# Expert weights in 8 KB pieces with permuted features, the long overflow block moved to the sixth pair, and cross attention outputs formed as columns

## The chip, the cores and the metric

One core of a Trainium2 chip runs the whole program in one launch. The metric is device time in microseconds (us); the time shown for a kernel is the median of its runs. Durations of single instructions and transfers come from one profiled execution of the same kernel.

## The reference, cut to what matters

Two blocks run on one sequence of 256 tokens with 1024 features. The first has two layers, each a mixer followed by a mixture of 16 experts; the second has two layers of mixer, cross attention to 256 memory tokens with 4 heads, and a dense feed-forward part. The change touches the experts and the cross attention:

```
scores = sigmoid(t @ router_w)                      # t: (256, 1024) normalised
# best group of 4 experts, top 2 inside it, weights normalised to 1
for e in range(16):
    he = silu(t @ w_gate[e]) * (t @ w_up[e])        # 1024 -> 512
    y = y + combine[:, e:e+1] * (he @ w_down[e])    # 512 -> 1024
# cross attention, per head of 64
p = softmax(q @ k.T * 0.125)                        # 256 x 256
o = p @ v                                           # 256 x 64
out = concat(o) @ ca_wo                             # 256 -> 1024
```

The expert weights are 2 layers x 16 experts x 6 MB in float32, 201 MB in all. The kernel may not choose tokens ahead of time: which tokens an expert gets is known only after the router.

## The kernel before, in words

x (two tiles of 128 tokens) stays in SBUF. Dense products use a high and a low part of each operand (tiles ending in h and l, or hi and lo); the expert products use plain float32. Every large weight is read by SP's queue (`fetch`, L220 and L221) into slots of 1 MB that are used in rotation; an expert stage has 17 of them.

`moe` (L1214) handles 16 experts as 8 pairs. The two experts of a pair stand side by side in the columns of TensorE, with 64 token places each. First the tokens are normalised (`xn`), split into `xh` and `xl` by ACT (L1255) and POOL (L1256), and scored and ranked on DVE (L1271 to L1318). `prepare` makes, for two pairs at once, one-hot rows (`kept`, DVE, L1340) and gathers the tokens by products with xh and xl (`ph`, L1352); ACT applies the layer's scale and shift per feature (`hg`, L1356, with A and B, tiles moda and modc). `up(p)` multiplies by gate and up (`pg` and `pu`, L1399, 32 records each), scatters the pair before it back into x (`py`, L1419 and L1420, through `self.pending`; DVE adds at L1422), computes where its own tokens go (`places`: `pS`, `pw`, ACT L1372 and L1376), forms silu(pg) * pu on ACT and DVE (`hd`, L1407), transposes it on TensorE (`hT`, L183) and copies it out on DVE (`hidT`, L1412). For p = 1, 3, 5 it then prepares the next two pairs. `down(p)` multiplies by the down weights (`po`, L1432), scales on DVE (`of`, L1444) and splits for the scatter (`eo`, ACT L1447, DVE L1448).

Per pair, twelve transfers of 1 MB are issued (`weights`, L1520): four for gate, four for up, four for down. A piece is what one partition takes in one run of memory: with "(k p) n -> p k n" a row at a time, 2 KB for gate and up (rows of 512 values), 4 KB for down (rows of 1024).

An expert may get more than 64 tokens. From the third pair on, `If` blocks (L1545 and L1548) take up to 32 more per expert; `rounds` (L1509 to L1516) is five nested blocks for still more, thousands of instructions, and jumps over all of them for this data. It stands at p == 7, between the issue of pair 7's gate and up weights and that of its down weights, on PE, DVE, ACT and SP (L1511; the count is loaded at L1532). The order on each engine is the order of the code, apart from what a scheduler may move between pinned instructions.

`cross` (L2095) forms scores per head, exp on ACT (L2133), reciprocals of the sums (L2134), transposes P (`cpT`, copied to `pT` by ACT L196 or DVE L198), and multiplies with P transposed as the stationary side (`co`, L2154): rows of tokens, 64 columns per head. Then DVE scales by the reciprocal (`e`, L2158), `rows_T` transposes the result (`trr`) and splits it (ACT L630, DVE L631), and the output product follows (`op`, L380 to L382).

Of the kernel before, what the change touches and what calls it, by code (L numbers as in the profile page):

```python
# [119 lines left out]
class Net:  # L120
# [99 lines left out]
    def fetch(self, raw, src):  # L220
        self.nc.sync.dma_start(raw, src.rearrange("(k p) n -> p k n", p=P))  # L221
        return raw
# [973 lines left out]
    def router(self, l):  # L1196

        nc = self.nc
        V = nc.vector
        A, B = self.scale_shift(l, 1)  # L1200
        rwa = self.sp.tile([P, KD, NE], F32, tag="gt", name="rwa")
        self.rwp = self.sp.tile([P, KD, 2, NE], F32R, tag="e1", name="rwp")
        V.tensor_tensor(rwa, self.rw, A.unsqueeze(2).to_broadcast([P, KD, NE]), op=ALU.mult)
        hi, lo = self.rwp[:, :, 0, :], self.rwp[:, :, 1, :]
        self.tc.keep_in_program_order(nc.scalar.copy(hi, rwa))
        V.tensor_tensor(lo, rwa, hi.bitcast(F32), op=ALU.subtract)
        rwb = self.sp.tile([P, KD, NE], F32, tag="gt", name="rwb")
        V.tensor_tensor(rwb, self.rw, B.unsqueeze(2).to_broadcast([P, KD, NE]), op=ALU.mult)
        V.tensor_reduce(self.rb, rwb.rearrange("p k e -> p e k"), axis=AX.X, op=ALU.add)
        pb = self.bank([P, NE], name="rb")  # L1210
        nc.tensor.matmul(pb, self.k("ones"), self.rb, start=True, stop=True)
        V.tensor_copy(self.rb, pb)

    def moe(self, l):  # L1214
# [4 lines left out]
        with self.phase(f"moe{l}", MOE_RING, True) as mp:  # L1219
# [124 lines left out]
            def gather(oh, hg, k0=0, k1=KD):  # L1344
# [3 lines left out]
                for b0 in range(k0, k1, per):  # L1348
# [5 lines left out]
                    for b in range(per):  # L1354
                        k = b0 + b
                        nc.scalar.activation(hg[:, k, :], ph[:, b, :], AF.Identity,  # L1356
                                             scale=A[:, k:k + 1], bias=B[:, k:k + 1])
# [27 lines left out]
            def up(p, W):  # L1385
# [38 lines left out]
            def down(W, hidT, Sm, ws, last=False):  # L1424
# [13 lines left out]
                def back(n=4):  # L1438
# [20 lines left out]
            def more_up(p, r, W, hidT):  # L1459
# [22 lines left out]
                for k in range(4):  # L1482
                    self.tr(pt[:, k, :], hd[:, 128 * k:128 * k + 128])
# [25 lines left out]
            def rounds(r):  # L1509

                with tc.If(left > 32 + 32 * r):  # L1511
                    for rr, pp in [(1, e) for e in range(FIRST if r == 2 else 0)] + [(r, e) for e in range(8)]:
                        hidT = self.sp.tile([P, 4, 64], F32, tag="e2", name="hidTa")
# [6 lines left out]
            def weights(src, step, p, into=None):  # L1520
# [4 lines left out]
                t = [self.fetch(raw, w[j][k0:k0 + step, :]) for raw, (j, k0) in zip(into, cut)]  # L1525
                return t[0::2], t[1::2]

            for p in range(8):
                W = [weights("exp_w_gate", 512, p), weights("exp_w_up", 512, p)]
                self.spare = [self.slot([P, 2048]) for i in range(4)]  # L1530
                if p == 7:
                    left = nc.values_load(cnti[0:1, 0:1], min_val=0, max_val=2 * S,  # L1532
                                          engines=engines + (mybir.EngineType.SP,))
                    rounds(2)
                W.append(weights("exp_w_down", 256, p, self.spare))
# [559 lines left out]
    def cross(self, l):  # L2095
# [3 lines left out]
        with self.phase(f"ca{l}") as ap:  # L2099
# [9 lines left out]
            o = [self.bank([P, 256], name=f"co{t}") for t in range(2)]  # L2109
            rs = ap.tile([P, 2, 4], F32, name="rs4")  # L2110
# [11 lines left out]
            def scores(m):  # L2122
# [4 lines left out]
                for h, ps in zip((2 * m, 2 * m + 1), pp):  # L2127
# [6 lines left out]
                    V.reciprocal(rs[:, :, h], sm)  # L2134
                    st[h] = p

            def turned(m):
                for h in (2 * m, 2 * m + 1):
                    pt = self.bank([P, 2, 2, P], name="cpT")
                    for t in range(2):  # L2140
                        for j in range(2):
                            self.tr(pt[:, t, j, :], st[h][:, t, 128 * j:128 * j + 128])
                    st[h] = ap.tile([P, 2, 2, P], F32, tag="pT", name="pT", bufs=4)
                    self.copy(st[h], pt)

            def out(m):
# [9 lines left out]
            for t in range(2):  # L2156
                oo = self.sp.tile([P, 512], F32, tag="e1", name="e1")
                V.tensor_tensor(oo[:, 0:256].rearrange("p (h d) -> p h d", h=4), o[t].rearrange("p (h d) -> p h d", h=4),  # L2158
                                rs[:, t, :].unsqueeze(2).to_broadcast([P, 4, 64]), op=ALU.mult)
                self.rows_T(oo[:, 0:256], oT, 0, 2, t)  # L2160
                self.fill(2)
# [181 lines left out]
```

## Time and profile before

| what | value |
|---|---|
| median of 3 runs | 1603.82 us (1601.02 to 1606.61) |
| profiled execution | 1602.07 us, span 1600.3 us |
| PE busy | 1504.7 us, 94% |
| DVE, ACT, POOL busy | 887.1, 679.6, 121.4 us |
| weights' queue | 403.46 MB, 71.1% of the 16 engines' span |
| first expert stage | about 200 to 468 us |
| second expert stage | about 605 to 857 us |
| cross attention's ends | about 1024 to 1045 and 1381 to 1400 us |

A page row names the line, the engine and the operation, then output and inputs, the count, the busy time, the mean of one in ns, and the idle time of that engine ahead of it with what ended it. PE records overlap, so their busy times can add up to more than the stretch; where one engine's next instruction starts is the safer number.

### The profile page before, as it was taken

Reading aid. Unit: us, or ns where it says so; the run is one execution under the profiler, and the core shown is the slowest. Engines: PE = TensorE matmul, PEld = TensorE weight load, DVE = VectorE, ACT = ScalarE, POOL = GpSimd, SP = SyncE. Lnnn points to the kernel's source line nnn. Section 1 sums busy time; section 2 is a strip of 40 time slices with the busy share of each in tenths; the row PEclk is TensorE's granted clock in tenths of the full one; section 3 lists DMA queues with packets and bytes.
Section 4 is the critical chain, followed back from the end, with each engine's and each line's share of the span. In section 5 each row is a group of like instructions: output and inputs, shape, how many; then the busy total and the mean of one; then the engine's idle time right before and its main releaser. Section 6 shows DMA issues by size and latency. Waiting matters only on the chain. (4 is left out here: it accounts for less than half of the span.)

```text
span 1600.3 us, 23014 instructions
## 1 busy us (share of the span) xinstructions
PE 1504.7 (94%) x8845; PEld 1072.0 (67%) x8845; DVE 887.1 (55%) x1704; ACT 679.6 (42%) x1421; POOL 121.4 (8%) x170
## 2 busy tenths in 40 slices
PE   6999999999789999999978999999999999999998
PEld 3766644444349975444425887888887997888887
DVE  3755531122248984222116786766667776766666
ACT  3434421111035653101105355665556666665554
POOL 0320010000000002000001100110000211110000
PEclk9999999999889999999989999999999999999999
DMA  9998999989968799999998632554655542545640
GB/s 357 345 314 294 344 396 391 391 315 393 347 215 273 276 328 366 397 391 392 394 340 277 182 106 93 162 194 162 220 171 161 163 150 84 186 157 186 210 158 27
DMA packets 225758, 412.30 MB, mean 258 GB/s; under 512 B 7705, under 2 KB 91313, under 8 KB 225617
## 3 DMA queue, kind: packets, MB, share of 16 engines
q1 hardware_dynamic: 223040, 403.46, 71.1%
q0 software_dynamic: 2304, 6.98, 1.4%
q8 instruction: 86, 1.41, 0.4%
q14 instruction: 56, 0.45, 0.1%
q10 hardware_dynamic: 272, 0.00, 0.0%
HBM read 409.35 MB, written 1.06 MB: 256 GB/s over the span
## 5 line engine op out<-in xcount | busy, mean ns | idle before, releaser
L229 DVE TENSOR_TENSOR hl<-w,hl 128x1024 fp32r<-128x1024 f32 x280 | 337.2, 1237 | 49.8 <-ACT hl L228 49.4
L228 ACT CAST hl<-w 128x1024 fp32r<-128x1024 f32 x280 | 280.3, 1046 | 33.0 <-DMA w<-in_even_w_in 19.6
L2218 PE MATMUL pgu<-hT,hl 128*128 128x512 f32 x640 | 224.3, 394 | 0.0
L2219 PE MATMUL pgu<-hT,hl 128*128 128x256 f32 x640 | 177.1, 277 | 0.0
L380 PE MATMUL lin<-hl,hThi 128*128 128x256 f32 (+2 forms) x480 | 158.8, 334 | 2.0 <-ACT hl L228 1.3
L381 PE MATMUL lin<-hl,hThi 128*128 128x256 f32 (+2 forms) x480 | 153.6, 321 | 1.9 <-DVE hl L229 1.7
L382 PE MATMUL lin<-hl,hTlo 128*128 128x256 f32 (+2 forms) x480 | 153.1, 320 | 0.4 <-DVE hTlo L557 0.4
L2218 PEld LDWEIGHTS pgu<-hT,hl 128*128 128x128 f32 x640 | 119.9, 187 | 27.8
L1399 PE MATMUL pg<-w,hg 128*64 128x512 f32 x512 | 118.6, 615 | 19.7 <-ACTq L1545 9.2
L1407 DVE TENSOR_TENSOR hd<-hd,pu 128x512 f32<-128x512 f32 x16 | 11.0, 688 | 225.9 <-PE pu L1399 225.9
L1432 PE MATMUL po<-w,hidT 128*64 128x512 f32 x512 | 113.6, 595 | 10.0 <-DVEq L1548 5.8
L2219 PEld LDWEIGHTS pgu<-hT,hl 128*128 128x128 f32 x640 | 120.2, 188 | 2.0
L1399 PE MATMUL pu<-w,hg 128*64 128x512 f32 x512 | 114.9, 593 | 1.9 <-DMA w<-in_exp_w_up 1.9
L380 PEld LDWEIGHTS lin<-hl,hThi 128*128 128x128 f32 x480 | 92.3, 192 | 17.6 <-issue 8.1
L1399 PEld LDWEIGHTS pg<-w,hg 128*64 128x64 f32 x512 | 40.9, 141 | 93.4 <-issue 69.5
L381 PEld LDWEIGHTS lin<-hl,hThi 128*128 128x128 f32 x480 | 92.2, 192 | 11.0 <-DVE hl L229 3.5
L382 PEld LDWEIGHTS lin<-hl,hTlo 128*128 128x128 f32 x480 | 92.1, 192 | 8.0 <-issue 1.7
L1399 PEld LDWEIGHTS pu<-w,hg 128*64 128x64 f32 x512 | 41.1, 137 | 72.7 <-issue 68.0
L1432 PEld LDWEIGHTS po<-w,hidT 128*64 128x64 f32 x512 | 40.4, 137 | 72.8 <-issue 59.5
L1444 DVE SCALAR_TENSOR_TENSOR of<-po,ws,gate 128x512 f32<-128x512 f32 x32 | 23.9, 748 | 104.5 <-PE po L1432 100.6
L1447 ACT CAST eo<-of 128x512 fp32r<-128x512 f32 x32 | 19.8, 617 | 124.7 <-DVE of L1444 124.4
L380 PE MATMUL linc<-hThi,hl 128*128 128x256 f32 x224 | 66.8, 298 | 0.0
(554 smaller groups left out, 2915.0 us busy)
## 6 DMA issues: line engine op xcount, KB each, us to landing
w<-in_exp_w_gate SPq DMA_DIRECT2D x64, 1024.0 KB, 14.9
w<-in_exp_w_down SPq DMA_DIRECT2D x64, 1024.0 KB, 14.2
w<-in_exp_w_up SPq DMA_DIRECT2D x64, 1024.0 KB, 14.2
w<-in_ada_w SPq DMA_DIRECT2D x48, 1024.0 KB, 7.1
w<-in_ffn_wg SPq DMA_DIRECT2D x22, 1024.0 KB, 5.5
w<-in_ffn_wu SPq DMA_DIRECT2D x22, 1024.0 KB, 7.3
w<-in_ffn_wd SPq DMA_DIRECT2D x22, 1024.0 KB, 8.9
w<-in_even_w_in SPq DMA_DIRECT2D x14, 1024.0 KB, 10.1
```

What stands on the lines that cost most here:

```text
L228: pin(self.nc.scalar.copy(w[:, 0], src))
L229: pin(self.nc.vector.tensor_tensor(w[:, 1], src, w[:, 0].bitcast(F32), op=ALU.subtract))
L380: pin(mm(out, lh, rh, start=start, stop=False))
L381: pin(mm(out, lh, rl, start=False, stop=False))
L382: pin(mm(out, ll, rh, start=False, stop=stop))
L1399: pin(mm(pp[64 * j:64 * j + 64, :], hg[:, k, q][:, 64 * j:64 * j + 64], w[j][k // 4][:, k % 4, :], start=k == 0, stop=k == KD - 1, tile_po ...
L1407: V.tensor_tensor(hd, hd, pu, op=ALU.mult)
L1432: pin(mm(po[c][64 * j:64 * j + 64, :], hidT[:, k, 64 * j:64 * j + 64], W[2][j][k // 2][:, k % 2, 512 * c:512 * c + 512], start=k == 0, sto ...
L1444: V.scalar_tensor_tensor(of, po[c], ws, gate[:, cs], op0=ALU.mult, op1=ALU.mult)
L1447: nc.scalar.copy(eh[c], of)
L2218: mm(pp[i], wh[:, k, :], both[:, :, k, :], start=k == 0, stop=False)
L2219: mm(pp[i][:, 0, :], wl[:, k, :], hi[:, k, :], start=False, stop=k == KD - 1)
```

## The change

It has four parts. (1) The expert weights are read with "(p k) n -> p k n": a partition takes rows that follow one another, 8 KB in one piece, four rows of gate or up, two of down. So the order of the features along the partitions changes: xh and xl are written in that order by reads with a step of four, the scale and shift are laid out again through a DRAM tile `ab` by three POOL transfers, and the transposes of hd read with a step of two. (2) The scatter is split: two of its four products stand ahead of the transposes, two behind the copy, and `places` follows them. (3) `rounds` is called by `rest`, in pair 5 between the up and the down products, after gate and up of pair 6 have been issued; the order of the weight transfers is unchanged. (4) In the cross attention P is scaled by the reciprocal before it is transposed, V is the stationary side, and the output comes as columns (features on partitions) that are split at once by `finish`.

```diff
-    def fetch(self, raw, src):
-        self.nc.sync.dma_start(raw, src.rearrange("(k p) n -> p k n", p=P))
+    def fetch(self, raw, src, rows="(k p) n -> p k n"):
+        self.nc.sync.dma_start(raw, src.rearrange(rows, p=P))
...
+        flat = self.dram.tile([2, D], F32, name="ab")
+        for i, v in enumerate((A, B)):
+            nc.gpsimd.dma_start(flat[i].rearrange("(k p) -> p k", p=P), v)
+        self.ab = self.gp.tile([P, 2, 2, 4], F32, tag="ab", name="ab")
+        nc.gpsimd.dma_start(self.ab, flat.rearrange("i (b p k) -> p i b k", b=2, k=4))
...
-                    pin(nc.scalar.copy(xh[sl], xn[sl]))
-                    pin(nc.gpsimd.tensor_tensor(xl[sl], xn[sl], xh[sl].bitcast(F32), op=ALU.subtract))
+                    hi, lo = (e[sl].rearrange("p (k q) -> p k q", k=4) for e in (xh, xl))
+                    src = xn[sl].rearrange("p (q k) -> p k q", k=4)
+                    pin(nc.scalar.copy(hi, src))
+                    pin(nc.gpsimd.tensor_tensor(lo, src, hi.bitcast(F32), op=ALU.subtract))
...
                 if self.pending:
-                    self.pending()
-                Sm, ws = places([oh[t][:, q] for t in range(2)], p, 0)
+                    self.pending(2)
...
-                    self.tr(pt[:, k, :], hd[:, 128 * k:128 * k + 128])
+                    self.tr(pt[:, k, :], hd[:, 256 * (k // 2):256 * (k // 2) + 256].rearrange("p (q k) -> p k q", k=2)[:, k % 2, :])
                 hidT = self.sp.tile([P, 4, P], F32, tag="e2", name="hidT")
                 V.tensor_copy(hidT, pt)
+                if self.pending:
+                    self.pending(2)
+                Sm, ws = places([oh[t][:, q] for t in range(2)], p, 0)
...
+                t = [self.fetch(raw, w[j][k0:k0 + step, :], "(p k) n -> p k n") for raw, (j, k0) in zip(into, cut)]
...
+            def rest():
+                nonlocal left
+                W.extend(first_two(6))
+                self.spare = [self.slot([P, 2048]) for i in range(4)]
+                left = nc.values_load(cnti[0:1, 0:1], min_val=0, max_val=2 * S, engines=engines + (mybir.EngineType.SP,))
+                rounds(2)
...
                 own = up(p, W)
                 with tc.If(count > 64):
                     more_down(p, W, hidT, Sm, ws)
+                if p == 5:
+                    rest()
                 down(W, *own, p == 7)
...
-                    V.reciprocal(rs[:, :, h], sm)
+                    V.reciprocal(sm, sm)
+                    for t in range(2):
+                        V.tensor_scalar(p[:, t, :], p[:, t, :], sm[:, t:t + 1], None, op0=ALU.mult)
...
-                for h in (2 * m, 2 * m + 1):
-                    sl = slice(64 * h, 64 * h + 64)
-                    for t in range(2):
-                        for j in range(2):
-                            mm(o[t][:, sl], st[h][:, t, j, :], v[:, j, sl], start=j == 0, stop=j == 1)
+                o = self.bank([P, S], name="co")
+                for j in range(2):
+                    for b in range(2):
+                        h = 2 * m + b
+                        mm(o[64 * b:64 * b + 64, :], v[:, j, 64 * h:64 * h + 64], st[h][:, j, :], start=j == 0, stop=j == 1,
+                           tile_position=(0, 64 * b))
+                self.finish(oT, o, m)
```

PE in pair 6 of the first layer, from the up product to the branch ahead of the down product, before (pu is up, py the scatter, pS and pw the places, hT the transposes of hd):

```order
L1399 MATMUL pu<-w,hg 64x512 x16
L1419 MATMUL py<-eo,kept 128x512
L1420 MATMUL py<-eo,kept 128x512
...
L183 MATMUL pS<-kt,kept 128x128
L1365 MATMUL pw<-ch,kept 128x16
L1366 MATMUL pw<-cl,kept 128x16
...
L183 MATMUL hT<-kt,hd 128x128 x4
L1548 COMPARE_AND_BRANCH
```

The same stretch of PE in the changed kernel:

```order
L1409 MATMUL pu<-w,hg 64x512 x16
L1431 MATMUL py<-eo,kept 128x512
L1432 MATMUL py<-eo,kept 128x512
...
L183 MATMUL hT<-kt,hd 128x128 x4
L1431 MATMUL py<-eo,kept 128x512
L1432 MATMUL py<-eo,kept 128x512
...
L183 MATMUL pS<-kt,kept 128x128
L1375 MATMUL pw<-ch,kept 128x16
...
L1569 COMPARE_AND_BRANCH
```

The transposes moved from the end of the stretch to its middle; half of the scatter and the places now stand between them and the down product.

DVE in pair 5, before (kept is the one-hot rows for pairs 6 and 7, L1422 adds the scatter into x):

```order
L1407 TENSOR_TENSOR hd<-hd,pu 128x512
L1422 TENSOR_TENSOR x<-x,py 128x512 x4
L1340 TENSOR_TENSOR kept<-rk,kt 128x256 x2
L1412 COPY hidT<-hT 128x512
L1548 COMPARE_AND_BRANCH
```

and in the changed kernel:

```order
L1416 TENSOR_TENSOR hd<-hd,pu 128x512
L1434 TENSOR_TENSOR x<-x,py 128x512 x2
L1421 COPY hidT<-hT 128x512
L1434 TENSOR_TENSOR x<-x,py 128x512 x2
L1349 TENSOR_TENSOR kept<-rk,kt 128x256 x2
L1569 COMPARE_AND_BRANCH
```

The copy moved two additions ahead, and the one-hot rows now stand behind it.

PE behind the up part of pair 5 in the changed kernel (ph is the gather; L1569 is the small block, L1548 loads the count, L1523 is the long block):

```order
L1361 MATMUL ph<-kept,xl 128x256
L1569 COMPARE_AND_BRANCH
...
L1548 TENSOR_LOAD cnti
L1523 COMPARE_AND_BRANCH
...
L1523 UNCONDITIONAL_BRANCH x6
L1444 MATMUL po<-w,hidT 64x512 x16
```

Before, the small block was followed by the down product at once, and the long block stood behind the down product of pair 6.

## Rows read from the trace of the kernel before

**Rows 1.** The page: the up product's line, the gate weights' transfers.

```profile
L1399 PE MATMUL pu<-w,hg 128*64 128x512 f32 x512 | 114.9, 593 | 1.9 <-DMA w<-in_exp_w_up 1.9
...
w<-in_exp_w_gate SPq DMA_DIRECT2D x64, 1024.0 KB, 14.9
```

**Rows 2.** Windows: length, busy time of each engine, granted clock, DMA share, GB/s.

```profile
232.00:236.00 4.00, 4.00 (x22) 1.29 (x18) 0.00 (x0) 0.00 (x0) 0.00 (x0) 1.00 1.03 410
...
244.00:248.00 4.00, 4.00 (x22) 1.30 (x20) 0.00 (x0) 0.60 (x1) 0.00 (x0) 1.00 1.05 387
...
605.00:857.00 252.00, 227.95 (x1137) 106.11 (x1135) 67.97 (x130) 46.95 (x105) 7.52 (x8) 0.98 1.01 381
...
676.80:705.00 28.20, 27.07 (x128) 11.80 (x130) 8.05 (x13) 3.02 (x7) 0.00 (x0) 1.00 1.04 391
```

**Rows 3.** Timeline of PE, second expert layer, pairs 5 and 6: start, us, operation.

```profile
763.76 4.46 PE L1399 MATMUL pu<-w,hg 128*64 128x512 f32 x18
...
772.31 0.50 PE L1419 MATMUL py<-eo,kept 128*128 128x512 f32 x1
...
794.83 0.59 PE L1399 MATMUL pu<-w,hg 128*64 128x512 f32 x1
...
804.23 0.50 PE L1419 MATMUL py<-eo,kept 128*128 128x512 f32 x1
...
806.75 0.66 PE L183 MATMUL hT<-kt,hd 128*128 128x128 f32 x4
808.23 7.09 PE L1432 MATMUL po<-w,hidT 128*64 128x512 f32 x32 [0.83 <-DVEq L1548]
...
833.87 7.05 PE L1399 MATMUL pu<-w,hg 128*64 128x512 f32 x32
```

**Rows 4.** Timeline of ACT and PE around the long block, both layers.

```profile
435.49 9.48 PE L1399 MATMUL pg<-w,hg 128*64 128x512 f32 x32 [7.70 <-ACTq L1511]
...
816.52 0.62 ACT L1447 CAST eo<-of 128x512 fp32r<-128x512 f32 x1 [1.42 <-DVE of L1444]
...
824.53 9.52 PE L1399 MATMUL pg<-w,hg 128*64 128x512 f32 x32 [9.21 <-ACTq L1545]
```

**Rows 5.** Timeline of POOL, ACT and DVE at the first expert layer's start.

```profile
193.63 1.81 POOL L859 TENSOR_TENSOR x<-x,gt 128x512 f32<-128x512 f32 x1
...
199.92 1.13 ACT L1255 CAST xh<-xn 128x512 fp32r<-128x512 f32 x2
...
201.72 2.96 POOL L1256 TENSOR_TENSOR xl<-xn,xh 128x512 fp32r<-128x512 f32 x2
...
205.44 2.63 POOL L1256 TENSOR_TENSOR xl<-xn,xh 128x512 fp32r<-128x512 f32 x2 [0.76 <-ACT xh L1255]
205.58 1.36 DVE L1279 TENSOR_TENSOR ec<-sel 128x128 f32<-128x128 f32 x1
```

**Rows 6.** Timeline, first cross attention's end; last, instructions of L953 (ns min/median/max).

```profile
1034.32 3.82 PE L2154 MATMUL co<-kv,pT 128*128 128x64 f32 x32
...
1036.37 0.61 ACT L196 COPY pT<-cpT 128x512 f32<-128x512 f32 x1
...
1039.99 0.47 PE L380 MATMUL op<-hl,oTh 128*128 128x512 f32 x1
...
L953 DVE TENSOR_SCALAR p<-p,sm x64: 277/318/352, 142.5 to 991.6; 128x128 f32<-128x128 f32 x32, 128x256 f32<-128x256 f32 x32
```

**Rows 7.** Timeline of POOL ahead of the first expert layer.

```profile
192.37 3.07 POOL L859 TENSOR_TENSOR x<-x,gt 128x512 f32<-128x512 f32 x2 [60.94 <-DVE modc L793]
```

**Rows 8.** Timeline of PE and ACT, pair 5's gather; SP's waits, whole run.

```profile
775.96 0.39 PE L1352 MATMUL ph<-kept,xh 128*128 128x256 f32 x1 [0.47 <-DVE kept L1340]
...
777.31 4.03 ACT L1356 ACTIVATE hg<-ph,modc,moda 128x256 f32<-128x256 f32 x8 [1.78 <-PE ph L1352]
...
780.55 7.09 PE L1432 MATMUL po<-w,hidT 128*64 128x512 f32 x32 [0.40 <-ACT hg L1356]
...
SPq L1511 <- SPq L1511: 19.2, 4, 11.9
```

More of the change, by code (lines that the diff above doesn't have):

```diff
@@ L1356, in gather @@
                         nc.scalar.activation(hg[:, k, :], ph[:, b, :], AF.Identity,
-                                             scale=A[:, k:k + 1], bias=B[:, k:k + 1])
+                                             scale=self.ab[:, 0, k // 4, k % 4:k % 4 + 1],
+                                             bias=self.ab[:, 1, k // 4, k % 4:k % 4 + 1])
             def places(oh, p, r):
@@ L1436, in down, with back @@
                 order = [(c, t) for c in range(2) for t in range(2)]
-                def back(n=4):
+                def back(n):
                     for c, t in [order.pop(0) for i in range(n)]:
@@ L1482, in more_up @@
                 for k in range(4):
-                    self.tr(pt[:, k, :], hd[:, 128 * k:128 * k + 128])
+                    self.tr(pt[:, k, :], hd[:, 256 * (k // 2):256 * (k // 2) + 256].rearrange("p (q k) -> p k q", k=2)[:, k % 2, :])
                 nc.scalar.activation(hidT, pt[:, :, 0:64], AF.Silu)
@@ L1512, in rounds @@
                     for rr, pp in [(1, e) for e in range(FIRST if r == 2 else 0)] + [(r, e) for e in range(8)]:
-                        hidT = self.sp.tile([P, 4, 64], F32, tag="e2", name="hidTa")
                         more_down(pp, None, hidT, *more_up(pp, rr, None, hidT))
@@ L1524, in weights, with first_two @@
                 cut = [(j, k0) for k0 in range(0, w[0].shape[0], step) for j in range(2)]
-                t = [self.fetch(raw, w[j][k0:k0 + step, :]) for raw, (j, k0) in zip(into, cut)]
+                t = [self.fetch(raw, w[j][k0:k0 + step, :], "(p k) n -> p k n") for raw, (j, k0) in zip(into, cut)]
                 return t[0::2], t[1::2]
-            for p in range(8):
[L1529 to L1535, printed above, removed]
+            def first_two(p):
+                return [weights("exp_w_gate", 512, p), weights("exp_w_up", 512, p)]
+            def rest():
[4 more added lines that the diff above has]
+                rounds(2)
+            left, W = None, []
+            for p in range(8):
+                if p != 6:
+                    W = first_two(p)
+                    self.spare = None
+                W = W[-2:] + [weights("exp_w_down", 256, p, self.spare)]
                 if p == 7:
@@ L2108, in cross @@
             oT = ap.tile([P, 2, S], F32R, name="oTh"), ap.tile([P, 2, S], F32R, name="oTl")
-            o = [self.bank([P, 256], name=f"co{t}") for t in range(2)]
-            rs = ap.tile([P, 2, 4], F32, name="rs4")
             st = {}
@@ L2141, in turned @@
                         for j in range(2):
-                            self.tr(pt[:, t, j, :], st[h][:, t, 128 * j:128 * j + 128])
-                    st[h] = ap.tile([P, 2, 2, P], F32, tag="pT", name="pT", bufs=4)
-                    self.copy(st[h], pt)
+                            self.tr(pt[:, j, t, :], st[h][:, t, 128 * j:128 * j + 128])
+                    st[h] = ap.tile([P, 2, 2 * P], F32, tag="pT", name="pT", bufs=4)
+                    self.copy(st[h], pt.rearrange("p a b c -> p a (b c)"))
             def out(m):
@@ L2149, in out @@
                     self.split_ahead(4)
-                for h in (2 * m, 2 * m + 1):
-                    sl = slice(64 * h, 64 * h + 64)
-                    for t in range(2):
-                        for j in range(2):
-                            mm(o[t][:, sl], st[h][:, t, j, :], v[:, j, sl], start=j == 0, stop=j == 1)
-            self.pipe(2, (scores, turned, out), 2)
[L2156 to L2161, printed above, removed]
+                o = self.bank([P, S], name="co")
[5 more added lines that the diff above has]
+                self.finish(oT, o, m)
+            self.pipe(2, (scores, turned, out), 2)
             self.drain()
```

## The prediction

> **What bounds the kernel now.** I read the page's busy shares first, then windows over the expert stages, then the PE timeline pair by pair, and last ACT, DVE, POOL and SP at the places where PE stands still. PE is busy nearly all the span. The expert stages look different at first sight: in the second one the DMA share is 1.01 over 252 us [rows 2], so a reader would call it bound by the weights. The timeline corrects that. A stretch of 28.2 us inside it has PE busy 27.07 us beside a DMA share of 1.04: both are full, and what counts is who waits for whom. Stretches with gate/up traffic (2 KB pieces) move 387 GB/s, with down traffic (4 KB) 410 GB/s [rows 2]. A pair is 12.58 MB, so 32 us at the mean rate of 391; PE needs about 27.5 us of work for it. The transfers are therefore the slower side, but 17 slots are full when a layer starts, and the lead is eaten only at about 4.5 us per pair. The page's line of the up product has 1.9 us of waits for weights in all [rows 1], and the timeline places them in the second layer: the up product of pair 5 lasts from 763.76 to 772.31, 8.55 us, and of pair 6 from 794.83 to 804.23, 9.40 us, where the nominal product takes 7.05 [rows 3]: 1.50 + 2.35 = 3.9 us is all that weights cost in the expert layers. The other stops are a fixed wait of 0.83 us ahead of the down product for the transposed hidden rows [rows 3], the long block (9.21 us idle in the second layer, 7.70 in the first) [rows 4], the start of each layer, where DVE ranks while POOL splits [rows 5], and the end of each cross attention [rows 6].
>
> **The change part by part**, against the profiled execution (1602.07 us with 1600.3 of span; the median of the runs, 1603.82, stands 1.75 above it). Under 0.3%, 4.8 us, no difference can be told.
>
> *8 KB pieces.* Going from 2 to 4 KB raised the rate from 387 to 410. For 8 KB no row exists; the bounds are no gain over 2 KB (387) and another equal step (433). I take 420: a pair then takes 30 us, and the lead is eaten at 2.5 us per pair, 15 us over six pairs, half of what was eaten before. So PE stops waiting for weights: **-3.9 us**, and not more, because no other PE wait in these layers is for a weight. At the lower bound gate and up are no faster and the gain is 0. (The Trainium skill, DMA: Bandwidth & Descriptors, in its warning on three rates, lets the HBM side bind at about 358 GB/s for a core, whatever the piece. By it the pieces could gain nothing and this term would be 0. The trace disagrees: 410 was moved [rows 2].)
>
> *Strided reads at a layer's start.* xh and xl are now written from reads with a step of four elements: four ACT casts (0.56 us each) and four POOL subtractions (1.48 each, then 1.32) [rows 5]. The POOL pass counts, since DVE's ranking operations end when POOL's do: 1.36 us for 128x128, from 205.58 on. No strided POOL row exists. Bounds: nothing, and the slowest POOL pass of this size, 1.81 us [rows 5]. At 1.81 the first two end at 201.72 + 3.62 = 205.34, before the next pair starts; the next end at 205.44 + 3.62 = 209.06 instead of 208.07: +1.0 us on the path. ACT between 0 and twice its time, where two casts stand ahead of the router's cast: 0 to +1.1. I take +1.0 a layer, because the steps are small beside a POOL pass of over a microsecond: **+2.0 us** (0 to +4.2). (The Trainium skill, GPSIMD Engine Reference, Performance pitfalls for Q7 kernels, speaks against this edit: it charges reads with a byte step over 8 about half more per element. The step here is 16 bytes. By it the passes would take 2.2 and 2.0 us, POOL would end near 210.1, and this term would be about +4; no run here shows it yet.)
>
> *Transposes with a step of two.* Four per pair take 0.66 us [rows 3]. Bounds 0 and doubled, +0.66 x 16 = +10.6 us; I take 0, because what is strided is the stationary side, loaded beside the running product.
>
> *Three small POOL transfers per layer* (scale and shift to DRAM and back in the new order). POOL stands idle for 60.94 us ahead of L859 [rows 7], where they now stand, and their reader is the gather at 210, so 0. Without that cover a landing of microseconds would sit ahead of the router.
>
> *Order inside a pair.* Before: up product, four scatters, places, transposes, copy (PE waits 0.83), down product. After: two scatters, transposes, two scatters, places. The copy (0.69 us on DVE) now runs under two scatters and the places, which are 1.5 us of PE work. PE's way from 804.23 to 808.23 is 4.00 us; without the wait it is 2.52 (to the transposes at 806.75) + 0.66 = 3.2: -0.75 in pairs 2, 4, 6, 7, and about -0.5 in pair 0, where only the places are moved under the copy. In pairs 1, 3, 5 the gather of the next pair covers the copy already. There it costs: DVE's one-hot rows, for which the gather waits at 775.96 (0.47 us) [rows 8], now stand behind the copy, 0.65 us later. Per layer -4 x 0.75 - 0.5 + 3 x 0.65 = -1.55; both **-3.1 us**. Bounds: -5 if the one-hot rows are not late, +0.5 if the copy is late by both x additions.
>
> *The long block in pair 5 instead of ahead of pair 7.* It is never executed, but each engine jumps over it and must fetch code. Before, PE waited for ACT: in the second layer ACT ends its last cast at 816.52 + 0.62 = 817.14 and PE resumes at 824.53, 7.4 us later; the first layer's stop is 9.21 - 7.70 = 1.5 shorter behind the same work, so about 5.9 [rows 4]. After, PE's down product of pair 5 stands behind the block and waits for ACT again. ACT's last work ahead of it is the gather's scaling, which ends at 777.31 + 4.03 = 781.34, 0.8 after the time 780.55 at which the down product started [rows 8]. So the stop is 0.8 + 5.9 to 7.4, less 0.4 that was waited there anyway: 6.3 to 7.8. I take 7.7, against (7.70 + 9.21) / 2 = 8.45: **-1.5 us** for both layers (-4.5 to +2). SP stands 11.9 us at the block [rows 8]; a weight takes 14.9 us from issue to landing [rows 1], so its queue stays filled, and the lead at pair 5 covers the rest.
>
> *Cross attention.* Removed: 32 product records, 3.82 us, and behind them scaling, transposes, cast and subtraction, until the output product starts at 1039.99 [rows 6]. Added: eight scalings of P on DVE (0.35 us each, by the self attention's L953 [rows 6]), a cast and a subtraction per head pair. The last copy of P transposed is ACT's, from 1036.37 to 1036.98, behind other casts, so the last head's two scalings, 0.7 us ahead of its transposes, can be absorbed. Then come 8 records of 256 columns (about 0.9 us) to 1037.9. The output product can start with the first head pair's rows and meets the second's in time: 1037.8 instead of 1039.99, -2.2; two of them: **-4.4 us** (-6.5 if the last copy comes earlier, -1 if the scalings lie on the path).
>
> Sum: -3.9 + 2.0 - 3.1 - 1.5 - 4.4 = -10.9. 1602.07 - 10.9 = 1591.2 for a profiled execution, 1592.9 against the median: **1593 us**.
>
> **The rivals.**
> - *The expert layers are bound by transfers after all.* For it: share 1.01 to 1.04. Against it: PE busy 27.07 of 28.2. If so, 100.7 MB a layer at 420 instead of 391 would save 17 us a layer: 1603.8 - 34 - 4 = about 1566. Chance 0.04.
> - *Code fetch in mid-stream (slower).* In pair 5 the pages of the jump come through the same DMA engines as 8 KB pieces; before they met 2 KB pieces. Place: ACT's jump at the block. Price: from nothing (5.9 and 7.4 us, code fetched while weights were moving) to four times the wait, +18 us a layer; in the middle +9, which gives 1593 + 18 = 1611. It turns the change into no gain at +5.5 a layer and makes it slower beyond 0.3% from +7.9 on. Chance 0.14.
> - *The pieces give nothing and the strides cost the upper bound.* 0 + 4.2 - 3.1 - 1.5 - 4.4 = -4.8: 1599; with half the cross gain swallowed by the next stage's weight conversion 1601. For it: most terms are under 5 us and the pieces help only in two pairs of one layer. Chance 0.20.
> - *The forecast* keeps 0.62.
>
> **How the numbers follow.** Faster by over 0.3%: forecast and transfers, 0.66. Same: 0.20. Slower: 0.14. Range: the low end takes most of the bounds in favour (-5 pairs, -4.5 block, -6.5 cross, no stride cost, about -20): 1583. The high end goes through the no-gain rival into the lower part of the code-fetch one: 1606.
>
> **What would show it.** Right: no idle time of PE put down to an up weight; the wait of 0.83 us gone in pairs 2, 4, 6, 7; a stop of 7 to 8 us inside pair 5 and none before pair 7; the output product of the cross about 2.2 us earlier after the last P copy; rates near 420 GB/s in the gate/up windows. Wrong: POOL's xl passes at over 2 us with the gather's start 2 us later; jumps of over 12 us; transposes of over 1.2 us per pair; a weight wait in pairs 6 and 7 behind SP's stop.

## The result, and the profile of the changed kernel

The changed kernel takes 1620.62 us (median, 1617.97 to 1623.11); the kernel before, on the same chip, 1603.31. The ratio is 1.0112 with a 95% interval of [1.0099, 1.0126]: slower by about 17 us, where 10 us faster was forecast and 1606 was the end of the range. The profiled execution has a span of 1621.3 us, 21.0 more than before; it is the slowest of its four, so the table shows about 4 us more than the medians do.

Where the 21 us lie is seen by setting the same events of both timelines side by side:

| event (start, us) | before | after | later by |
|---|---|---|---|
| POOL's x addition ahead of the first expert layer | 192.37 | 200.99 | 8.6 |
| first gate product of that layer | 212.83 | 225.35 | 12.5 |
| end of its last down product | 462.87 | 474.07 | 11.2 |
| POOL's x addition ahead of the second expert layer | 601.83 | 628.63 | 26.8 |
| first gate product of that layer | 622.27 | 649.82 | 27.6 |
| end of its last down product | 851.95 | 873.47 | 21.5 |
| end of the span | 1600.3 | 1621.3 | 21.0 |

The expert layers' pairs gain, 1.3 us in the first and 6.0 in the second. Everything that is lost is lost in the two mixers ahead of them (8.6, and 26.8 - 11.2 = 15.6) and at the starts of the layers (3.9 and 0.8). The cross attentions, which were to gain 4.4, leave almost nothing in the last row.

Into the mixers the change puts POOL's three transfers per layer, and the larger pieces of the expert weights that are fetched early. The timeline of POOL in the changed kernel (start, us, operation, idle time ahead and what ended it); the first x addition answers to [rows 7]:

```profile
109.31 0.94 POOL L1204 DMA_DIRECT2D ab<-moda  x1
...
140.01 0.94 POOL L1204 DMA_DIRECT2D ab<-modc  x1
154.27 0.77 POOL L1206 DMA_DIRECT2D ab<-ab  x1 [13.31 <-DMA ab<-modc]
200.99 3.07 POOL L859 TENSOR_TENSOR x<-x,gt 128x512 f32<-128x512 f32 x2 [45.95 <-DVE modc L793]
...
555.55 0.96 POOL L1204 DMA_DIRECT2D ab<-moda  x1 [70.80 <-DVE moda L796]
587.04 0.91 POOL L1204 DMA_DIRECT2D ab<-modc  x1 [30.54 <-DVE modc L787]
599.36 0.77 POOL L1206 DMA_DIRECT2D ab<-ab  x1 [11.41 <-DMA ab<-modc]
```

POOL itself has time to spare, 45.95 us, as forecast. But a transfer of 4 KB takes 13 and 11 us to come back. What the DMA engines did meanwhile is in the windows of the changed kernel from 109 us on (length, busy time of PE, PEld, DVE, ACT, POOL, granted clock, DMA share, GB/s):

```profile
109.00:113.00 4.00, 3.29 (x19) 2.52 (x17) 1.46 (x3) 3.80 (x6) 2.31 (x3) 1.00 1.01 373
113.00:116.00 3.00, 2.06 (x11) 1.81 (x12) 2.79 (x6) 2.20 (x5) 0.90 (x1) 1.00 1.42 245
116.00:119.00 3.00, 2.73 (x15) 1.09 (x13) 3.00 (x3) 0.00 (x0) 0.76 (x1) 1.00 1.05 29
119.00:122.00 3.00, 0.00 (x0) 0.00 (x0) 1.76 (x5) 0.00 (x0) 0.00 (x0) 1.00 1.09 87
122.00:125.00 3.00, 1.11 (x4) 0.19 (x4) 0.00 (x0) 0.00 (x0) 0.00 (x0) 0.76 0.75 228
125.00:128.00 3.00, 3.00 (x9) 1.47 (x9) 0.00 (x0) 0.00 (x0) 0.00 (x0) 0.67 1.04 387
```

The share is 1.05 and 1.09, and the queues together move 29 and 87 GB/s: for some eight microseconds, from 115 to 123, the weights hardly move, and the 4 KB written in 1024 pieces of 4 bytes is all that is new there (the number of pieces follows from the access pattern; the trace doesn't list them). The stretch as a whole, and below it ten microseconds of the kernel before at the same place:

```profile
115.00:123.00 8.00, 3.73 (x20) 1.91 (x18) 5.55 (x9) 0.81 (x3) 1.66 (x1) 1.00 1.03 61
...
110.00:120.00 10.00, 10.00 (x52) 5.65 (x51) 7.87 (x12) 4.62 (x8) 2.69 (x2) 1.00 1.03 372
```

The same share goes with 61 and with 372 GB/s, so a full share is not bandwidth in use. Here is the weights' queue (packets, MB, share), from 110 to 113 and from 116 to 119 us:

```profile
q1 hardware_dynamic: 593, 1.18, 102.9%
...
q1 hardware_dynamic: 50, 0.09, 104.8%
```

The same 16 engines' time holds 593 packets of weights, 0.08 us each, and then 50, of 1.0 us each. So the full share of the second stretch is the weights' own packets, each about twelve times as long. PE has no work from 119 to 122. The weights that come late are those of the modulation. In the first mixer PE waits for them itself, in the second DVE does, which does the modulation there, and PE behind DVE (timelines of PE, of DVE, of PE in the changed kernel):

```profile
123.89 1.92 PE L758 MATMUL ada<-w,cT 128*32 128x512 f32 x4 [5.16 <-DMA w<-in_ada_w]
```

```profile
568.04 0.49 DVE L761 TENSOR_SCALAR adarow<-w,cT 128x512 f32<-128x512 f32 x1 [7.05 <-DMA w<-in_ada_w]
...
599.01 0.49 DVE L761 TENSOR_SCALAR adarow<-w,cT 128x512 f32<-128x512 f32 x1 [6.32 <-DMA w<-in_ada_w]
```

```profile
569.71 0.39 PE L382 MATMUL linc<-hThi,hl 128*128 128x256 f32 x1 [3.93 <-DVE hl L229]
...
600.01 0.39 PE L1630 MATMUL z<-us,nuinc 128*128 128x256 f32 x1 [3.29 <-DVE us L203]
```

PE's idle time grows from 15.1 to 22.6 us in the first mixer and from 5.5 to 13.6 us in the second: 7.5 of the 8.6 us, and 8.1 of the 15.6. The mean granted clock falls too, from 1.00 to 0.97 and from 0.95 to 0.93. The rest of the 15.6 was not taken apart.

The expert layers did much of what the forecast said. The page and the windows of the changed kernel, beside [rows 1] and [rows 2]:

```profile
L1409 PE MATMUL pu<-w,hg 128*64 128x512 f32 x512 | 112.9, 592 | 0.0
```

```profile
200.00:204.00 4.00, 4.00 (x19) 3.28 (x19) 2.90 (x8) 0.73 (x2) 3.01 (x2) 1.00 1.00 422
256.00:260.00 4.00, 4.00 (x22) 1.33 (x20) 0.00 (x0) 0.60 (x1) 0.00 (x0) 1.00 1.00 414
```

No up weight is waited for, and 8 KB pieces move 414 to 422 GB/s (taken: 420). The long block's stops are now inside pair 5, beside [rows 4]; the wait of 0.83 us ahead of the down product [rows 3] is 0.30 in a pair that doesn't prepare (PE's timeline: pair 5 of either layer, then pair 7 of the second):

```profile
414.55 10.05 PE L1444 MATMUL po<-w,hidT 128*64 128x512 f32 x32 [4.36 <-PEq L1523]
...
814.03 9.98 PE L1444 MATMUL po<-w,hidT 128*64 128x512 f32 x32 [7.13 <-PEq L1523]
...
866.38 1.08 PE L1444 MATMUL po<-w,hidT 128*64 128x512 f32 x4 [0.30 <-DVE x L1434]
```

4.36 + 7.13 = 11.5 us stand where 7.70 + 9.21 = 16.9 stood. The product behind each stop takes 10 us instead of 7.09; the clock granted from 814 to 824 is 0.70 of full speed, a mean between its two levels of 1.2 and 2.4 GHz, after PE had stood still. The same was so in the kernel before (9.48 and 9.52 us) [rows 4].

### The profile page after: what moved, and what is told of

Same layout as the page of the kernel before. It is cut to its first block, busy times and chain, and to the rows that moved or that the text cites. A ratio compares the mean times of both kernels' runs of the same rounds, so it can differ in the third digit from the quotient of the medians.

```text
span 1621.3 us, 22921 instructions
## 1 busy us (share of the span) xinstructions
PE 1510.8 (93%) x8805; PEld 1076.0 (66%) x8805; DVE 890.9 (55%) x1716; ACT 684.5 (42%) x1421; POOL 128.3 (8%) x176
## 5 line engine op out<-in xcount | busy, mean ns | idle before, releaser
L2238 PEld LDWEIGHTS pgu<-hT,hl 128*128 128x128 f32 x640 | 119.8, 187 | 26.5
L1444 PE MATMUL po<-w,hidT 128*64 128x512 f32 x512 | 119.5, 620 | 15.3 <-PEq L1523 11.5
L1409 PE MATMUL pg<-w,hg 128*64 128x512 f32 x512 | 114.0, 596 | 3.4 <-PEq L1566 3.4
L1382 ACT CAST kept<-pS 128x256 fp32r<-128x256 f32 x17 | 6.3, 373 | 146.2 <-PE pS L183 146.2
## 6 DMA issues: line engine op xcount, KB each, us to landing
w<-in_exp_w_up SPq DMA_DIRECT2D x64, 1024.0 KB, 13.6
```

The costliest lines, as they stand in the source:

```text
L1409: pin(mm(pp[64 * j:64 * j + 64, :], hg[:, k, q][:, 64 * j:64 * j + 64], w[j][k // 4][:, k % 4, :], start=k == 0, stop=k == KD - 1, tile_po ...
L1444: pin(mm(po[c][64 * j:64 * j + 64, :], hidT[:, k, 64 * j:64 * j + 64], W[2][j][k // 2][:, k % 2, 512 * c:512 * c + 512], start=k == 0, sto ...
L2238: mm(pp[i], wh[:, k, :], both[:, :, k, :], start=k == 0, stop=False)
```

## The experiments

Theory: the 4-byte writes take the DMA engines from the weights, and that is the whole loss of the mixers. Rivals: the transfers are hidden, as forecast, and the 8 KB pieces, the block or the strides cost it. Times stand beside the kernel before on the same chip (1602.2 to 1602.5 us).

**1. The transfers alone.** The kernel before with these lines added; nothing reads `ab`.

```diff
+        flat = self.dram.tile([2, D], F32, name="ab")
+        for i, v in enumerate((A, B)):
+            nc.gpsimd.dma_start(flat[i].rearrange("(k p) -> p k", p=P), v)
+        self.ab = self.gp.tile([P, 2, 2, 4], F32, tag="ab", name="ab")
+        nc.gpsimd.dma_start(self.ab, flat.rearrange("i (b p k) -> p i b k", b=2, k=4))
```

> The kernel before, with nothing added but the three POOL transfers per layer that lay the scale and shift out again (two writes of 1024 pieces of 4 bytes to DRAM, one read back); their result is used by nothing. Theory: each of the two writes holds the DMA engines for about 10 us, the dense weights of the mixer come late, and PE stands for them; from the trace of the changed kernel this is 8.6 us in the first mixer and 15.6 in the second, so about 1603 + 24 = 1627 us (1618 to 1632). Rival (the forecast's own step: the transfers are hidden): 1603 within 3 us.

1629.17 us against 1602.38, ratio 1.0165 [1.0146, 1.0184]: +26.8 us. Three transfers of some kilobytes per layer cost more than the whole change loses. Its windows show the same stretch as the changed kernel's, with pieces of the old size, so 8 KB pieces have no part in it:

```profile
113.00:116.00 3.00, 1.49 (x9) 1.34 (x10) 2.77 (x6) 2.40 (x6) 0.34 (x1) 1.00 1.57 322
116.00:119.00 3.00, 3.00 (x18) 1.56 (x16) 3.00 (x4) 0.37 (x2) 1.32 (x1) 1.00 0.89 29
119.00:122.00 3.00, 0.31 (x1) 0.00 (x1) 2.33 (x5) 0.00 (x0) 0.00 (x0) 1.00 1.18 96
```

**2. The number of pieces.** As 1, but the same bytes go out as 128 pieces of 32 bytes.

```diff
-            nc.gpsimd.dma_start(flat[i].rearrange("(k p) -> p k", p=P), v)
+            nc.gpsimd.dma_start(flat[i].rearrange("(p k) -> p k", p=P), v)
```

> As the kernel with the three POOL transfers alone (1629 us), but each write to DRAM goes out in 128 pieces of 32 bytes instead of 1024 pieces of 4 (the same bytes, count of transfers and waits; the features then lie in another order, in a tile that nothing uses). Theory (the cost goes with the number of tiny pieces): two writes of about 10/8 us each per layer, at most +4 us, 1602 to 1606. Rival (the DRAM round trip and its waits on POOL's queue cost, whatever the pieces): 1620 or more.

1607.72 us against 1602.20, ratio 1.0031 [1.0021, 1.0040]: +5.5, a fifth of 26.8, with the same three transfers. A little over the expected 4. POOL's idle time ahead of the read back fell with it, from 12.7 and 11.8 us to 5.6 and 5.5. These windows of 3 us behind the first write don't fall below 227 GB/s:

```profile
108.00:111.00 3.00, 3.00 (x19) 2.52 (x16) 0.85 (x2) 2.80 (x4) 2.57 (x3) 1.00 1.00 340
111.00:114.00 3.00, 1.34 (x11) 1.00 (x10) 2.57 (x4) 2.50 (x4) 0.00 (x0) 1.00 1.06 400
114.00:117.00 3.00, 3.00 (x18) 2.24 (x20) 2.79 (x5) 1.20 (x3) 1.66 (x1) 1.00 1.03 383
117.00:120.00 3.00, 3.00 (x16) 0.99 (x9) 2.97 (x6) 0.00 (x0) 0.00 (x0) 1.00 0.75 227
```

So it is the tiny pieces that cost, not the round trip through DRAM. The run changes their number and their size together (and which pieces lie side by side in DRAM), and doesn't tell these apart.

**3. One write instead of two.** The kernel before with the scale's write alone, no read back.

```diff
+        flat = self.dram.tile([2, D], F32, name="ab")
+        for i, v in enumerate((A,)):
+            nc.gpsimd.dma_start(flat[i].rearrange("(k p) -> p k", p=P), v)
```

> The kernel before with one single write of 1024 pieces of 4 bytes per layer (the scale alone) and no read back; the result is used by nothing. Theory (each such write costs its 10 us of weights' transfer, and the path follows): half of the 26.8 us, 1614 to 1617. Rival (it is the wait of the read back on POOL's queue, or only the second write, that costs): 1602 to 1606.

1623.04 us against 1602.46, ratio 1.0135 [1.0110, 1.0160]: +20.6, three quarters and not half. The mechanism holds (no read back, no second write, and POOL's x addition still comes at 203.35 instead of 192.37, while in experiment 1 it came at 202.21), but the price is not per write. In the first mixer the first write costs everything and the second nothing: the second, at 141 us, falls where the weights have slack (208 GB/s from 150 to 160 us in the kernel before). In the second mixer the first costs about 10 us, and the second, with the read back, 4 more. What a stopped queue costs depends, by these places, on how soon PE needs what is in it.

**4. The change whole, laid out again without a transfer.** Sixteen small products (32 records in the trace) with columns of the identity bring scale and shift, which stand side by side in `both`, into the new order.

```diff
-        flat = self.dram.tile([2, D], F32, name="ab")
-        for i, v in enumerate((A, B)):
-            nc.gpsimd.dma_start(flat[i].rearrange("(k p) -> p k", p=P), v)
...
-        nc.gpsimd.dma_start(self.ab, flat.rearrange("i (b p k) -> p i b k", b=2, k=4))
+        eye = self.k("ident").rearrange("p (q k) -> p k q", k=4)
+        for g in range(4):
+            src = both.rearrange("p i (b g) -> p g i b", g=4)[:, g]
+            for k in range(4):
+                nc.tensor.matmul(pab[32 * g:32 * g + 32, :, :, k], eye[:, k, 32 * 0:32], src, start=True, stop=True,
+                                 tile_position=(0, 32 * g))
...
+        V.tensor_copy(self.ab, pab)
```

> The changed kernel whole, but scale and shift are laid out again by 16 small TensorE products with columns of the identity and one copy, with no transfer. Theory (the 4-byte writes cost 24 us): 1620.6 - 24 = about 1597 us (1592 to 1602), faster than the kernel before. Rival (8 KB pieces in the shared queue delay the mixers' weights, or the pieces are late themselves): 1612 us or more.

1600.26 us against 1602.38, ratio 0.9986 [0.9975, 0.9997]: 19 us better than the change, each against the kernel before on its own chip, and a little faster than before. The rival falls. But -2.1 is not the -10.9 of the forecast, so other terms were off too. The mixers now take 2.3 us (the first) and 1.4 us (the second) more than before instead of 8.6 and 15.6; of that the products are 1.45 us:

```profile
192.04 1.45 PE L1209 MATMUL pab<-both,kt 128*32 128x4 f32 x32
```

and the starts of the expert layers (from POOL's x addition to the first gate product) are 2.6 and 3.7 us longer. Two things make them longer. DVE, counted from the x addition, has its first one-hot rows ready 1.2 and 1.5 us later, because it waits longer for ACT, whose doubled casts stand ahead (first layer, before and here):

```profile
201.56 0.69 DVE L203 TENSOR_TENSOR hTlo<-tr,hThi 128x512 fp32r<-128x512 f32 x1 [0.44 <-ACT hThi L202]
...
204.82 0.69 DVE L203 TENSOR_TENSOR hTlo<-tr,hThi 128x512 fp32r<-128x512 f32 x1 [1.45 <-ACT hThi L202]
```

The other 3.6 us go with the clock. The windows of the first start, before, here, and with the long block alone (below), which changes nothing in a start:

```profile
192.37:212.83 20.46, 17.05 (x119) 12.31 (x117) 14.97 (x43) 8.64 (x22) 9.73 (x8) 1.00 1.04 395
194.71:217.72 23.01, 18.84 (x119) 13.32 (x117) 15.70 (x42) 10.61 (x22) 10.36 (x8) 0.93 1.01 422
193.20:215.01 21.81, 18.39 (x118) 13.23 (x116) 14.96 (x43) 8.64 (x22) 9.73 (x8) 0.92 1.04 395
```

A start at 0.92 is 1.4 us longer with nothing in it changed, and the second start here is at 0.87. Whether a start meets the lower level differs from one profiled execution to the next, and no run shows what decides it.

**5. The start of a layer.** As 4, but DVE, which writes the normalised tokens anyway, writes them in the new order, so ACT and POOL read without a step.

```diff
-                rs[t] = self.norm_rows(self.x, t, xn, t)
+                rs[t] = self.mean_square(self.x, t)
+                V.tensor_scalar(xn[:, t, :].rearrange("p (c k q) -> p c k q", c=2, k=4),
+                                self.x[:, t, :].rearrange("p (c q k) -> p c k q", c=2, k=4), rs[t], None, op0=ALU.mult)
...
-                    pin(nc.scalar.copy(hi, src))
-                    pin(nc.gpsimd.tensor_tensor(lo, src, hi.bitcast(F32), op=ALU.subtract))
+                    pin(nc.scalar.copy(xh[sl], xn[sl]))
+                    pin(nc.gpsimd.tensor_tensor(xl[sl], xn[sl], xh[sl].bitcast(F32), op=ALU.subtract))
```

> The kernel with all parts and scale and shift laid out on TensorE (1600.3 us), but DVE writes the normalised tokens in the permuted order, so ACT's casts and POOL's subtractions read without a step. Theory (ACT's doubled casts are what makes the start longer): casts back to 0.56 us, DVE's pass from 0.75 to at most 1.1 us, 1.5 us less per layer: 1597 (1595.5 to 1599). Rival (the start is longer for another reason, or DVE's pass takes what ACT gains): 1600 to 1602.

1596.20 us against 1602.20, ratio 0.9960 [0.9944, 0.9975]: 4 us better than experiment 4, where 3 were expected. The instructions of tile xn, first in the changed kernel, then in this one (count, ns min/median/max):

```profile
L1264 ACT CAST xh<-xn x8: 1099/1119/1132, 208.5 to 640.4; 128x512 fp32r<-128x512 f32 x8
L1265 POOL TENSOR_TENSOR xl<-xn,xh x8: 1502/1533/1771, 210.3 to 642.1; 128x512 fp32r<-128x512 f32 x8
```

```profile
L1268 ACT CAST xh<-xn x8: 602/610/615, 203.5 to 614.8; 128x512 fp32r<-128x512 f32 x8
L1269 POOL TENSOR_TENSOR xl<-xn,xh x8: 1292/1328/2179, 205.3 to 616.2; 128x512 fp32r<-128x512 f32 x8
L1274 DVE TENSOR_SCALAR xn<-x,rstd x4: 1197/1510/1852, 200.3 to 611.7; 128x1024 f32<-128x1024 f32 x4
```

ACT's cast takes 1.12 us with the step and 0.61 without; POOL's pass 1.53 and 1.33. DVE's two passes per layer became longer than expected: 1.20 and 1.8 us, where the kernel before took 0.75 and 1.4 (the second runs beside POOL). The whole still gains, but not all of the 4 us is shown to come from the casts. The first one-hot rows are ready 0.6 and 0.7 us earlier than in experiment 4. The two starts together are 4.9 us shorter; the other 3.6 go with the clock, which is 1.00 in both starts here. The run with the long block put back (below) has the same instructions at its starts, 0.92 in both, and 1.4 us more in each. Over whole runs the granted clock was 0.980 to 0.983 here and 0.976 to 0.980 in experiment 4; that the edit raised it isn't shown.

**6. The products in PE's idle time.** As 5, with the sixteen products moved from ahead of the mixer's output products to the start of the expert layer, where PE waits for the ranking; ACT copies the result.

```diff
             self.warm(WARM[2])
+            pab = self.bank([P, 2, 2, 4], name="pab")
...
             parts(1)
+            self.ab = self.gp.tile([P, 2, 2, 4], F32, tag="ab", name="ab")
+            pin(nc.scalar.copy(self.ab, pab))
```

> As the kernel in which DVE writes the permuted order (1596.2 us), but the 16 small TensorE products that lay scale and shift out stand in the expert layer's start, where TensorE waits for the ranking, and ACT copies their result; before, they stood ahead of the mixer's output products and took 1.6 us of TensorE there. Theory: 1.6 us less per layer, 1593 us (1592 to 1595). Rival (they are not on the path, or they delay the ranking's products): 1596 or more.

1592.79 us against 1602.46, ratio 0.9931 [0.9916, 0.9946], as expected (1593): 9.7 us faster than the kernel before, 27 faster than the change (each against the kernel before on its own chip), and the best version of this study. That all of the 3.4 us against experiment 5 come from the move isn't shown; the two intervals touch.

**7 to 11. The parts by themselves.** The cross attention alone (the last three pieces of the diff, in the kernel before):

> The kernel before with the cross attention's part of the change alone. The forecast: -4.4 us (1599). Theory from the trace of the changed kernel (the last head's two scalings wait behind two copies on DVE, and its transposes behind products of the other heads, so the output product gains 0.6 us in the first cross and not 2.2): -0.5 to -3 us (1600 to 1603).

1600.98 us, ratio 0.9988 [0.9978, 0.9999]: -1.4 of the forecast -4.4. Its timeline, beside [rows 6]:

```profile
1035.37 0.67 DVE L198 COPY pT<-cpT 128x512 f32<-128x512 f32 x1
1035.96 0.61 DVE L2134 TENSOR_SCALAR p<-p,sm 128x256 f32<-128x256 f32 x2
...
1036.45 0.41 PE L183 MATMUL cpT<-kt,p 128*128 128x128 f32 x2 [1.15 <-DVE p L2134]
1036.79 1.51 PE L2155 MATMUL co<-pT,kv 128*64 128x256 f32 x10
1038.23 0.44 PE L183 MATMUL cpT<-kt,p 128*128 128x128 f32 x2
1038.71 0.59 ACT L196 COPY pT<-cpT 128x512 f32<-128x512 f32 x1 [0.41 <-PE cpT L183]
1039.34 1.08 PE L2155 MATMUL co<-pT,kv 128*64 128x256 f32 x6 [0.68 <-ACT pT L196]
...
1040.35 0.50 PE L380 MATMUL op<-hl,oTh 128*128 128x512 f32 x1
```

The last head's scalings stand on DVE behind two copies of earlier heads, PE waits 1.15 us for them, and the last two transposes stand on PE behind ten records of the product. In the forecast these lay under ACT's late copy. From ACT's last copy to the output product it is 1.64 us, where [rows 6] have 3.62, so that part of the forecast (-2.2) nearly came; but the copy itself comes later by PE's wait.

The long block alone (`rest` called in pair 5, pieces as before):

> The kernel before with the long block moved into pair 5 alone, pieces and order within a pair unchanged. The forecast: -1.5 us. Theory from the trace of the changed kernel (stops of 4.0 and 6.8 us in pair 5 instead of 7.7 and 9.2 ahead of pair 7): -4 to -6 us (about 1598). Rival (code pages wait behind weights, SP's stop leaves the weights of pairs 6 and 7 late): slower than 1603.

1601.09 us, ratio 0.9991 [0.9980, 1.0002]: -1.3, near the forecast's -1.5, a gain that the interval doesn't quite separate from none. The stops were not the 4.0 and 6.8 us that were expected from the changed kernel:

```profile
404.60 8.97 PE L1432 MATMUL po<-w,hidT 128*64 128x512 f32 x32 [7.40 <-PEq L1511]
...
790.36 8.94 PE L1432 MATMUL po<-w,hidT 128*64 128x512 f32 x32 [7.34 <-PEq L1511]
```

14.7 us against 16.9 before: so the move alone shortens the stops by 2.2 us, and the first layer's short stop of 4.36 us comes only together with the rest of the change. Up weights were waited for longer, 4.1 us on the page's line of the up product against 1.9 [rows 1]: in the second layer, where weights are late, the shorter stops gained nothing (229.65 us from the first gate to the last down product, against 229.68). That a shorter stop gives late weights less time to catch up fits this, and is not tested by itself. So the other way round, from experiment 5 with the block put back:

```diff
+                if p == 7:
+                    left = nc.values_load(cnti[0:1, 0:1], min_val=0, max_val=2 * S,
+                                          engines=engines + (mybir.EngineType.SP,))
+                    rounds(2)
...
-                if p == 5:
-                    rest()
```

> As the kernel in which DVE writes the permuted order (1596.2 us), but the long block is back ahead of pair 7. Theory (moving the block gives about 3 us once the weights are early, in stops of 12 us in all against about 15): 1599 (1598 to 1601). Rival (the move alone gave 1.1 us, and gives no more here): 1596 to 1597.5.

1598.78 us against 1596.20 with the block in pair 5 (ratio to before 0.9970 [0.9958, 0.9981]): with weights that are early the move is worth 2.6 us, though the two intervals overlap. The stops agree: 6.74 + 7.87 us here, 4.76 + 7.19 in experiment 5, 2.7 us less.

The order within a pair alone (scatter in halves, places last):

> The kernel before with the order inside a pair alone (scatter in two halves around the transposes and the copy, places last). The forecast: -3.1 us, 1599. Theory after the runs so far (in the second expert layer the weights are late, so what PE saves in a pair it waits for at the next one; only the first layer keeps its share): -1 to -2 us, 1600 to 1601.5. Rival (DVE's one-hot rows behind the copy cost more than the wait that goes): 1603 or more.

1601.22 us, ratio 0.9988 [0.9978, 0.9997]: -1.0. PE's way from the end of the up product to the down product shows it pair by pair, and alike in both layers: 3.33 us instead of 3.94 in pairs 2, 4, 6 and 7, 2.33 as before in pair 0, and 0.6 more in pairs 1, 3 and 5 (8.3 to 8.8 instead of 7.7 to 8.2), where the one-hot rows come later. That adds up to -0.6 us a layer, -1.2 in all. It was expected that late weights take the second layer's part back; they do not: the up products of pairs 5 and 6 in the second layer, where PE waits for weights, take 17.8 us together, against 18.1 before.

The pieces and the permuted features alone, laid out again on PE as in 4:

> The kernel before with the 8 KB pieces and permuted features alone, scale and shift laid out again on TensorE. The forecast's terms: -3.9 + 2.0 = -1.9, 1600.5. Theory from the kernel with all parts (the start of an expert layer became 2 to 4 us longer, ACT's casts with a step of four took 1.07 us each instead of 0.56; the second layer gains from the pieces): -3.9 + 2 x 2.6 + 1 for the products that lay out = +2, about 1604 (1601 to 1606). In the trace no wait for an up weight.

1607.93 us against 1602.20, ratio 1.0031 [1.0015, 1.0046]: +5.7, slower, and more than the +2 expected. The second layer's pairs gain 4.2 us (225.5 against 229.7), as the forecast's -3.9. The starts of the layers lose 3.8 and 2.2 us, the mixers 3.6 and 1.5, the first layer's pairs 1.5. Of the mixers' part the products are 1.5 us each. Much of the rest goes with the clock in this profiled execution: it was at the lower level from 26.0 to 29.4 us, where the kernel before has none of it; at the starts it was 0.86 and 0.92, against 1.00; and the 1.5 us of the first layer lie where the small block runs, between pairs 2 and 3 (26.5 us at a mean of 0.81, against 24.9 at 0.86).

## Why the prediction was wrong

- *Three small POOL transfers: 0.* This step failed, and it alone turned the sign. The forecast costed the edit by POOL's idle time (60.94 us, [rows 7], which was right) and by when the reader comes. It did not ask what the transfer does to the other users of the DMA engines, and it set no bounds. Measured by itself: +26.8 us; as part of the change about 19 (the change against experiment 4, which has its own small products instead). The Trainium skill, DMA: Bandwidth & Descriptors, Specifications, gives 512 bytes as the smallest transfer for full rate and says that smaller ones are read, modified and written. The runs agree as far as they go: with 4-byte pieces all queues together move 29 to 87 GB/s. But 32-byte pieces, also below 512, cost only a fifth of the 26.8 us, and no run shows the reading and writing back.
- *8 KB pieces: -3.9.* Right: 414 to 422 GB/s, no wait for an up weight, the pairs of the second layer 4.2 us shorter; the up products of pairs 5 and 6, which the forecast had put at 3.9 us too long, take 7.06 us each with the pieces alone.
- *Strided reads: +2.0 (0 to 4.2).* The size was near, by the wrong engine, so partly by luck. The ranking ends 1.2 + 1.5 = 2.7 us later (experiment 4). The forecast watched POOL; it was ACT, which takes its upper bound, twice its time: 1.12 - 0.61 = 0.5 us more for each of four casts, two of them ahead of the router's cast, for which DVE waits 1.45 us instead of 0.44. The starts as a whole grew by 6.3 us; the other 3.6 go with the granted clock, for which the forecast had no term, and which also falls where no read has a step. The figure that the forecast set beside this term, half more by the Trainium skill (GPSIMD Engine Reference, Performance pitfalls for Q7 kernels), is not borne out by this pass: 1.53 against 1.33 us is 15% more.
- *Transposes with a step of two: 0.* Nearly right; the stationary load took 0.21 us instead of 0.14, four times a pair, and PE's way to the down product grew by 0.09 us in pairs 2, 4, 6 and 7 with the pieces alone.
- *Order inside a pair: -3.1.* The mechanism is right (in pair 7 from the scatter's start to the down product 3.45 us instead of 4.01), the size is not: -1.0 alone. A pair without a gather gained 0.6 us and not 0.75, and pair 0 nothing instead of 0.5. The gather's wait for the one-hot rows in pair 5 grew from 0.47 [rows 8] to 1.10 us, as forecast.
- *The long block: -1.5.* About right: -1.3 alone, -2.6 with early weights. The code-fetch rival is out: no stop became longer with 8 KB pieces; in pair 5 they are 4.36 and 7.13 us, with 2 KB pieces 7.40 and 7.34. Why the first is so much shorter was not tested.
- *Cross: -4.4.* A third of it, -1.4. The forecast bound the gain by PE and ACT and took the scalings as absorbed; they stand in DVE's queue, and PE waits 1.15 us for them.

Together: -2.1 for the whole without the transfers, and the writes on top. The four parts measured alone add up to -1.4 - 1.3 - 1.0 + 5.7 = +2.0, 4 us off the whole; each is known to about 2 us, so whether the parts add stays open. Of the rivals none had the right mechanism; the slower one was placed at the wrong transfer.

## What to carry to other kernels

A small transfer is priced at the engines that all queues share, not at the queue that issues it: count its pieces, and ask whose weights stand behind them and how soon they are needed. A layout that a few small TensorE products can make needs no trip through DRAM; put them where PE waits anyway, and let the engine that writes the data first also write it in the new order. Savings in a stage that waits for its weights are not simply added up: the shorter stops of the long block gained nothing in the layer whose weights were late. And before a stretch of one profile is put down to an edit, its granted clock is set beside that of the other profile: a start of the same instructions was 1.4 us longer at 0.92.

## What the runs showed that was not expected

One write of 4 KB in 1024 pieces kept the share of the sixteen DMA engines at 1.03 for about eight microseconds (115 to 123), in which all queues moved 61 GB/s, where 387 were moved right after; a packet of weights took 1.0 us instead of 0.08. A step of 16 bytes in an ACT read nearly doubled a cast (0.61 to 1.12 us) and lengthened DVE's scaling passes by 0.4 us each (0.75 to 1.20, 1.4 to 1.8), while POOL's pass rose by 15%. And the price of the same stopped queue went from nothing to 10 us, by what stood in it.
